# One step of a hybrid decoder layer on one core: x turned once and kept turned in DRAM, banded scores as stacked float32r products

## The chip, the cores and the metric

The kernel runs on one core of a Trainium2 chip. Its metric is the device time of one execution in microseconds (us); 0.2% of it, 3.9 us, is about what a measurement of this kernel can tell from no change. Engines: TensorE (PE) multiplies, and its weight loads are shown as PEld; VectorE (DVE) and ScalarE (ACT) do the elementwise work; GpSimd (POOL) and SyncE (SP) mostly issue DMAs. A Tile scheduler fixes the order of the instructions on each engine before the run, so each engine works strictly through its own list.

## The reference, cut to what matters

A prompt of 256 tokens and a sample group of 8 tokens go through one layer with the same weights (width 2048):

```python
def _rmsnorm(x, g):
    y = x * lax.rsqrt(jnp.mean(jnp.square(x), axis=-1, keepdims=True) + EPS)
    return y * g
# each layer
h = _rmsnorm(x, norm_mix)
q, k, v, z, xbc, dt, qm, g = jnp.split(h @ w_in, ...)
# branch A: window attention, 16 query heads of 64, 4 key/value heads, blocks of 128 positions
s = einsum('...qhgd,...khd->...hgqk', q, k) * 64 ** -0.5   # 128 queries x (previous + own block) keys
s = where(allowed, s - slopes * dist, -inf)
p = softmax with a learned sink per head
o = einsum('...hgqk,...khd->...qhgd', p, v)
# branch B: Mamba-2 SSD with a convolution; branch M: attention into 256 memory tokens
x = x + (sig(gA) * A @ w_up_swa + sig(gB) * B @ w_up_ssd + sig(gM) * M @ w_up_mem) @ w_out
x = x + (silu(h2 @ w_gate) * (h2 @ w_up)) @ w_down,   h2 = _rmsnorm(x, norm_ffn)
```

x is thus needed twice: normalized, as the input of the projections, and raw, in the residual sum after w_out.

## The kernel before

Features lie on the 128 partitions and tokens on the free axis: NT = 264 columns, 256 of the prompt (NP) and 8 of the samples (NS). The weights stream through in **units** of 512 KB, 610 of them. For each unit SP loads `raw`, ACT rounds it to float32r (`hi`, L167), DVE takes the remainder (`lo`, L168), and PE adds three float32r products for each tile of 128 features by 128 outputs, named after the PSUM bank that they fill: high by high, high by low, low by high. There are three buffers of `hi` and of `lo` and four of `raw`, so a unit is split up to three units before its products. A unit of 264 columns has 24 products.

The groups of units follow each other in the order in which they are added: memory keys and values (`pmem`, 32 units with products of 512 columns), then the input projection (`pin`): memory queries, attention queries, keys and values, gates of the memory branch, B, C, dt, then x and z of the four SSD groups between the first output projections (`pua`), then `pum`, the SSD gates, `pus`, `pout` (w_out), and the feed-forward part (`pg`, `pu`, `pdn`).

All other work is written as generators, the side tasks. After each unit the main loop lets the list `side` go on by a credit of 1.0 and the list `slow` by 0.75; each `yield` takes its number from that credit. So the numbers at the yields set at which unit a task's instructions are placed in program order; `drain` finishes a task at once where a group needs it. Program order is the scheduler's priority. Three pieces matter here:

- `prep_x` (L402 to L442) loads x, normalizes rows and turns them: for each of the 16 feature tiles k, PE turns two blocks of 128 prompt tokens and one of 8 sample tokens into PSUM (`xT`), ACT writes the high part `hh` (L439), DVE the low part `hl` (L440).
- `swa` (L785 on) computes the prompt's attention. For block 1 (256 keys) and block 0 (128 keys) and for each pair of key/value heads, PE forms scores `ps` from 64 partitions of q and of the keys kT in plain float32 (L836), DVE scales and masks them, ACT takes exponents, PE turns the probabilities (`pT`), ACT copies them to `pTa`, and PE multiplies with the values into `po` (L873): one product of 512 columns for each half a of the pair, into 64 PSUM partitions each. A plain float32 product is two PE instructions in the trace, one float32r product is one.
- `load_x` (L1447) runs ahead of each of the four `pout` groups: it loads x again, turns it again on PE (`xTr`) and copies it with ACT, for the residual sum in `after_out`.

Buffers: the pool `half` has 10 large tiles, `t1` 4 tiles of 264 columns, `ev` 4, `t4` 4; PSUM has 5 banks for the streamed groups and 3 (`sps`) for side work.

Of the kernel before, what the change touches and what calls it, by code (L numbers as in the profile page):

```python
# [8 lines left out]
F32 = mybir.dt.float32  # L9
# [9 lines left out]
P = 128  # L19
# [53 lines left out]
def tile_hybrid_decoder_step(  # L73
# [68 lines left out]
    def sps(name):  # L142
        return pq.tile([P, 512], F32, tag="s", name=nm(name))

    def mm(out, lhsT, rhs, start=True, stop=True):
        nc.tensor.matmul(out, lhsT=lhsT, rhs=rhs, start=start, stop=stop)  # L146

    def tr(out, in_):
        n = in_.shape[0]
        nc.tensor.transpose(out, in_, ident[0:n, 0:n])  # L150

    def rsqrt(v, n, parts=P, alloc=None):

# [246 lines left out]

    hh, hl = Feat("hh"), Feat("hl")

    def prep_x():
        x_t = {}
        for h in range(2):
            for t in range(2):
                m = (lm if t else ld)("x")
                nc.gpsimd.dma_start(m, x_prompt[0, t * P:(t + 1) * P, h * 1024:(h + 1) * 1024])
                x_t[t, h] = m
                yield 1.3  # L410
        xs = {h: ev("xs").rearrange("p c n -> p (c n)")[0:NS, 0:1024] for h in range(2)}
        for h in range(2):
            nc.gpsimd.dma_start(xs[h], xs_rows[:, h * 1024:(h + 1) * 1024])
            x_t[2, h] = xs[h]
        jk = t2("jkx", BF16)
        ss = tiny("ssx", 6)
        V.memset(ss, 1.0)
        for t in range(3):
            n = P if t < 2 else NS
            for h in range(2):  # L420
                act(jk[0:n], x_t[t, h], AF.Square, accum_out=ss[0:n, 2 * t + h:2 * t + h + 1])
            yield 0.5
        v = tiny("vx", 3)
        V.tensor_tensor(v, ss[:, 0:6:2], ss[:, 1:6:2], op=ALU.add)
        V.tensor_scalar(v, v, 1.0 / D, EPS, op0=ALU.mult, op1=ALU.add)
        r = rsqrt(v, 3)
        yield 1.5
        for t in range(3):
            n = P if t < 2 else NS
            for h in range(2):  # L430
                V.tensor_scalar(x_t[t, h], x_t[t, h], r[0:n, t:t + 1], None, op0=ALU.mult)
            yield 1.2
        for k in range(KT):
            ps = sps("xT")
            h, c = k // 8, (k % 8) * P
            for t in range(3):
                n = P if t < 2 else NS
# [351 lines left out]
    def swa():  # L789
# [33 lines left out]
        V.tensor_tensor(rq[:, 32:33], rq[:, 32:33], islope_c, op=ALU.mult)  # L823
        yield 3

        for blk in (1, 0):
            nk = 256 if blk else 128
            for kvp in range(2):
                halves = [slice(a * 64, a * 64 + 64) for a in range(2)]
                s = [t4("s")[:, 0:4 * nk].rearrange("p (r k) -> p r k", r=4) for _ in range(2)]  # L830
                per = 512 // nk
                for j in range(4 // per):
                    ps = [sps("ps").rearrange("p (r k) -> p r k", r=per) for _ in range(2)]
                    for i in range(per):
                        for a, rows in enumerate(halves):
                            mm(ps[a][:, i], q[rows, 4 * kvp + j * per + i, blk * P:(blk + 1) * P], kT[rows, kvp, 0:nk])  # L836
                    for a in range(2):
                        for i in range(per):
                            rr = j * per + i
                            o = blk * 16 + (2 * kvp + a) * 4 + rr  # L840
                            V.scalar_tensor_tensor(s[a][:, rr], ps[a][:, i], rq[:, o:o + 1], nd[:, 256 - nk:256],
                                                   op0=ALU.mult, op1=ALU.add)
                    yield 2.2 if blk else 2.8
                for a in range(2):
                    kv = 2 * kvp + a
                    hs = slice(kv * 4, kv * 4 + 4)
                    mx = tiny("mxa", 8)
                    V.tensor_reduce(mx[:, 0:4], s[a], axis=AX.X, op=ALU.max)
                    V.tensor_tensor(mx[:, 0:4], mx[:, 0:4], nslope[:, hs], op=ALU.mult)
                    V.tensor_tensor(mx[:, 0:4], mx[:, 0:4], nsink[:, hs], op=ALU.min)  # L850
# [12 lines left out]
                po = sps("po")  # L863
                for kb in range(nk // P):
                    pT = []
                    for a in range(2):
                        p2 = sps("pT")
                        for rr in range(4):
                            tr(p2[:, rr * P:(rr + 1) * P], s[a][:, rr, kb * P:(kb + 1) * P])
                        pT.append(t2("pTa"))  # L870
                        act(pT[a], p2, AF.Copy)
                    vb_ = blk - (nk // P - 1) + kb
                    for a, rows in enumerate(halves):  # L873
                        kv = 2 * kvp + a
                        mm(po[rows, 0:512], v_tok[:, vb_, kv * 64:(kv + 1) * 64], pT[a],
                           start=kb == 0, stop=kb == nk // P - 1)
                    yield 0.4
# [567 lines left out]
    x2 = {}  # L1445

    def load_x(i):  # L1447
        xt = t4("xg")[:, 0:1024].rearrange("p (t c) -> p t c", t=2)
        nc.gpsimd.dma_start(xt, x_prompt[0, :, 512 * i:512 * (i + 1)].rearrange("(t p) c -> p t c", p=P))
        xs = t2("xgs")[0:NS]  # L1450
        nc.gpsimd.dma_start(xs, xs_rows[:, 512 * i:512 * (i + 1)])
# [175 lines left out]
```

## Time and profile before

| what | value |
|---|---|
| median of 3 runs | 1950.66 us (1947.3 to 1951.65) |
| the profiled execution, its own time | 1951.31 us |
| its span in the trace | 1949.6 us |
| PE busy | 1927.4 us (99%), 15436 instructions |
| weight loads busy | 1863.8 us (96%) |
| DVE busy | 1160.9 us (60%) |
| ACT busy | 972.0 us (50%) |
| POOL busy | 115.2 us (6%) |
| HBM traffic | 205 GB/s over the span |

Busy times are unions over an engine's instructions. Products overlap in the pipeline, so a PE that is busy all the time may still move at different rates; the distance from start to start tells what a product takes. The span is 1.7 us shorter than the profiled execution's time.

### The profile page before, as it was taken

How to read it: one execution, taken by the hardware profiler on the slowest of the kernel's cores; microseconds unless marked ns; L12 is line 12 of the kernel's file. 1: busy time of each engine (PE TensorE's matmuls, PEld its weight loads, DVE VectorE, ACT ScalarE, POOL GpSimd, SP SyncE). 2: the span in 40 equal slices, each digit the busy share in tenths (PEclk: the TensorE clock that was granted, in tenths of full speed). 3: DMA queues.
4: the chain of work that ended last, by engine and by line, in shares of the span. 5: the costliest groups of instructions: out<-in, count | busy, mean ns of one | idle time of the engine just before them, and what ended most of it. 6: DMA issues, size and time to landing. Idle time of an engine off the chain costs nothing.

```text
span 1949.6 us, 37668 instructions
## 1 busy us (share of the span) xinstructions
PE 1927.4 (99%) x15436; PEld 1863.8 (96%) x15436; DVE 1160.9 (60%) x2217; ACT 972.0 (50%) x1420; POOL 115.2 (6%) x238
## 2 busy tenths in 40 slices
PE   8999999999999999999999999999999999999998
PEld 6799998888999999999999999999999999999998
DVE  6645577656588777677455556555445555445553
ACT  6644445655767676646444444444334444334443
POOL 3000100010001101020000000000000000000000
PEclk9999999999999999999999999999999999999999
DMA  8676676567668869788655556666566665566653
GB/s 285 195 218 207 205 221 228 184 212 244 199 201 254 285 190 320 250 294 281 180 190 188 189 163 174 183 175 185 183 182 178 182 182 180 180 183 178 181 188 128
DMA packets 191030, 400.78 MB, mean 206 GB/s; under 512 B 13443, under 2 KB 15794, under 8 KB 190720
## 3 DMA queue, kind: packets, MB, share of 16 engines
q1 hardware_dynamic: 169856, 324.13, 54.6%
q0 software_dynamic: 20848, 74.16, 11.6%
q8 instruction: 121, 1.98, 0.4%
q14 instruction: 53, 0.43, 0.1%
q10 hardware_dynamic: 152, 0.07, 0.0%
HBM read 376.53 MB, written 24.06 MB: 205 GB/s over the span
## 4 chain that ended last, share of the span: by engine, by line
PE 89%; DMA 4%; issue 3%; DVE 2%; ACT 1%; POOL 0%; SPq 0%; ACTq 0%; POOLq 0%; DVEq 0%
PE pin L146 26%; PE pu L146 13%; PE pdn L146 13%; PE pg L146 13%; PE pout L146 5%; PE pus L146 5%; PE pmem L146 5%; PE pua L146 2%; PE pum L146 1%; DMA ld<-in_state_ssm_dram 1%; PE po L146 1%; PE py L146 1%; PE ps L146 1%; DMA ld<-in_cache_mem_v_dram 1%; DMA ld<-in_cache_mem_k_dram 1%
## 5 line engine op out<-in xcount | busy, mean ns | idle before, releaser
L168 DVE TENSOR_TENSOR lo<-raw,hi 128x1024 fp32r<-128x1024 f32 (+1 forms) x626 | 747.3, 1196 | 624.5 <-ACT hi L167 623.2
L167 ACT ACTIVATE hi<-raw 128x1024 fp32r<-128x1024 f32 (+1 forms) x626 | 645.9, 1036 | 846.4 <-PE pin L146 185.5
L146 PE MATMUL pin<-hh,hi 128*128 128x264 f32 x1728 | 491.0, 287 | 2.7 <-ACT hi L167 2.7
L146 PE MATMUL pin<-hl,hi 128*128 128x264 f32 x1728 | 489.9, 286 | 0.0
L146 PE MATMUL pin<-hh,lo 128*128 128x264 f32 x1728 | 479.2, 286 | 0.7 <-DVE lo L168 0.7
L146 PEld LDWEIGHTS pin<-hh,hi 128*128 128x128 f32 x1728 | 325.2, 189 | 9.3 <-issue 4.8
L146 PEld LDWEIGHTS pin<-hl,hi 128*128 128x128 f32 x1728 | 325.3, 188 | 2.8 <-issue 2.2
L146 PEld LDWEIGHTS pin<-hh,lo 128*128 128x128 f32 x1728 | 319.1, 188 | 3.6 <-DVE lo L168 1.9
L146 PE MATMUL pdn<-fah,hi 128*128 128x264 f32 x704 | 199.7, 285 | 0.0
L146 PE MATMUL pdn<-fal,hi 128*128 128x264 f32 x704 | 199.4, 285 | 0.0
L146 PE MATMUL pu<-h2h,hi 128*128 128x264 f32 x704 | 199.4, 284 | 0.0
L146 PE MATMUL pu<-h2l,hi 128*128 128x264 f32 x704 | 199.3, 284 | 0.0
L146 PE MATMUL pg<-h2l,hi 128*128 128x264 f32 x704 | 199.1, 285 | 0.0
L146 PE MATMUL pg<-h2h,hi 128*128 128x264 f32 x704 | 198.4, 284 | 0.0
L146 PE MATMUL pdn<-fah,lo 128*128 128x264 f32 x704 | 197.0, 284 | 0.0
L146 PE MATMUL pu<-h2h,lo 128*128 128x264 f32 x704 | 196.6, 284 | 0.0
L146 PE MATMUL pg<-h2h,lo 128*128 128x264 f32 x704 | 196.1, 284 | 0.0
L146 PEld LDWEIGHTS pdn<-fah,hi 128*128 128x128 f32 x704 | 132.7, 189 | 0.1
L146 PEld LDWEIGHTS pu<-h2h,hi 128*128 128x128 f32 x704 | 132.8, 189 | 0.0
L146 PEld LDWEIGHTS pdn<-fal,hi 128*128 128x128 f32 x704 | 132.6, 188 | 0.1
L146 PEld LDWEIGHTS pu<-h2l,hi 128*128 128x128 f32 x704 | 132.7, 188 | 0.0
L146 PEld LDWEIGHTS pg<-h2h,hi 128*128 128x128 f32 x704 | 132.6, 188 | 0.0
(509 smaller groups left out, 2957.5 us busy)
## 6 DMA issues: line engine op xcount, KB each, us to landing
raw<-in_w_in_dram SPq DMA_DIRECT2D x218, 512.0 KB, 4.6
raw<-in_w_gate_dram SPq DMA_DIRECT2D x88, 512.0 KB, 3.8
raw<-in_w_up_dram SPq DMA_DIRECT2D x88, 512.0 KB, 4.4
raw<-in_w_down_dram SPq DMA_DIRECT2D x88, 512.0 KB, 4.1
raw<-in_w_mem_kv_dram SPq DMA_DIRECT2D x32, 512.0 KB, 4.9
raw<-in_w_up_ssd_dram SPq DMA_DIRECT2D x32, 512.0 KB, 3.8
raw<-in_w_out_dram SPq DMA_DIRECT2D x32, 512.0 KB, 3.6
ld<-in_cache_mem_k_dram POOLq DMA_DIRECT2D x16, 512.0 KB, 5.6
```

Source lines behind the costliest of these rows:

```text
L146: nc.tensor.matmul(out, lhsT=lhsT, rhs=rhs, start=start, stop=stop)
L167: act(hi, src, AF.Copy)
L168: V.tensor_tensor(lo, src, hi.bitcast(F32), op=ALU.subtract)
```

## The change

**x.** `prep_x` loads the 8 sample rows as one tile of 128 partitions (16 feature tiles by 8 rows) and turns that once (`xn`). Their sums of squares come from a product with a small selection matrix in the same PSUM bank. The raw prompt blocks are turned as before, two for each feature tile, and ACT copies them into `xr`, which holds raw turned x. The norm is now applied along the columns: `rb`, the reciprocal norms spread over all partitions by a product of ones with a diagonal (`rbx`), enters a DVE operation that makes `xn`; ACT then takes `hh` and DVE `hl` from it. Each `xr` (4 feature tiles) is stored to DRAM (`xT_d`), and `load_x` reads it back with one DMA, without PE and ACT.

**Attention of the prompt.** Before the scores, the keys are split in high and low parts, and each part is copied onto both halves of the partitions (`kst`). The queries of each half are split too: the high part stays on its own 64 partitions, the low part goes to the other 64 (`qst`, one tile for each half). A score tile is then two float32r products over 128 partitions, one with the high and one with the low keys, in place of one float32 product over 64 partitions. The turned probabilities of both halves now share a PSUM bank and one copy, and each value product covers 256 columns.

```diff
-        for h in range(2):
-            nc.gpsimd.dma_start(xs[h], xs_rows[:, h * 1024:(h + 1) * 1024])
+        xs = t1("xs")[:, 0:P]
+        nc.gpsimd.dma_start(xs, xs_rows.rearrange("b (k n) -> k b n", n=P))
...
+        ps = sps("xn")
+        tr(ps[:, 0:P], xs)
+        mm(ps[:, P:P + NS], ones, sel)
...
+        mm(ps[:, 0:NP], ones, dg)
+        rb = t1("rb")
...
-            for t in range(3):
-                n = P if t < 2 else NS
-                tr(ps[:, t * P:t * P + n], x_t[t, h][:, c:c + P])
-            act(hh(k), ps[:, 0:NT], AF.Copy, scale=g_mix[:, k:k + 1])
-            V.scalar_tensor_tensor(hl(k), ps[:, 0:NT], g_mix[:, k:k + 1], hh(k).bitcast(F32),
-                                   op0=ALU.mult, op1=ALU.subtract)
-            yield 0.4
+                for t in range(2):
+                    tr(ps[:, t * P:(t + 1) * P], x_t[t, h][:, o:o + P])
+                act(raw[:, c, 0:NP], ps[:, 0:NP], AF.Copy)
+                tm = t1("xn")
+                V.scalar_tensor_tensor(tm, raw[:, c], g_mix[:, k:k + 1], rb, op0=ALU.mult, op1=ALU.mult)
+                split(hh(k), hl(k), tm)
+                yield 0.6
+            nc.gpsimd.dma_start(xT_d[:, 4 * q:4 * q + 4], raw)
...
+        kst = half("kst", F32R)
+        for a in range(2):
...
+            split(kh[own], kl[own], src)
+            V.tensor_copy(kh[other], kh[own])
+            V.tensor_copy(kl[other], kl[own])
+            yield 1.0
+        qst = [half("qst", F32R) for _ in range(2)]
+        for kvp in range(2):
+            for a in range(2):
...
+                act(d[own], src, AF.Copy)
+                V.tensor_tensor(d[other], src, d[own].bitcast(F32), op=ALU.subtract)
+                yield 0.8
...
-                            mm(ps[a][:, i], q[rows, 4 * kvp + j * per + i, blk * P:(blk + 1) * P], kT[rows, kvp, 0:nk])
+                            for m in range(2):
+                                mm(ps[a][:, i], qst[a][:, 4 * kvp + j * per + i, blk * P:(blk + 1) * P],
+                                   kst[:, 4 * m + 2 * kvp + a, 0:nk], start=m == 0, stop=m == 1)
...
+                for rp in range(2):
+                    for kb in range(nk // P):
                         p2 = sps("pT")
+                        for a in range(2):
+                            for r2 in range(2):
+                                o = (2 * a + r2) * P
+                                tr(p2[:, o:o + P], s[a][:, 2 * rp + r2, kb * P:(kb + 1) * P])
+                        pT = t2("pTa")
+                        act(pT, p2, AF.Copy)
...
+                            mm(po[rows, 256 * rp:256 * rp + 256], v_tok[:, vb_, kv * 64:(kv + 1) * 64],
+                               pT[:, 256 * a:256 * a + 256], start=kb == 0, stop=kb == nk // P - 1)
+                        yield 0.4
...
-        for c in range(4):
-            ps = sps("xTr")
-            for t in range(2):
-                tr(ps[:, t * P:(t + 1) * P], xt[:, t, c * P:(c + 1) * P])
-            tr(ps[:, NP:NT], xs[:, c * P:(c + 1) * P])
-            act(o[:, c], ps[:, 0:NT], AF.Copy)
+        nc.gpsimd.dma_start(o, xT_d[:, 4 * i:4 * i + 4])
```

How the order of the instructions changes at three places. First PE, where the first `pout` group follows the last `pus` group; before:

```order
L146 MATMUL pus_12332<-sT_9950,lo_12450 128x264
L150 MATMUL xTr_12599<-ident,xg_12594 128x128 x2
L150 MATMUL xTr_12599<-ident,xgs_12596 128x8
L150 MATMUL xTr_12604<-ident,xg_12594 128x128 x2
L150 MATMUL xTr_12604<-ident,xgs_12596 128x8
L150 MATMUL xTr_12609<-ident,xg_12594 128x128 x2
L150 MATMUL xTr_12609<-ident,xgs_12596 128x8
L146 MATMUL pout_12619<-mg_11766,hi_12479 128x264 x2
```

and now, at the same place:

```order
L146 MATMUL pus_12447<-sT_10065,hi_12564 128x264 x2
L146 MATMUL pus_12447<-sT_10065,lo_12565 128x264
L146 MATMUL pout_12711<-mg_11881,hi_12594 128x264 x2
L146 MATMUL pout_12711<-mg_11881,lo_12595 128x264
L146 MATMUL pout_12712<-mg_11881,hi_12594 128x264 x2
```

The transposes are gone, here and in the other three groups. Second PE, where value products and scores of block 1 stand between `pin` products; before:

```order
L146 MATMUL pin_3503<-hh_112,lo_3410 128x264
L146 MATMUL po_3374<-pTa_3387,v_tok_2746 64x512
L150 MATMUL pT_3398<-ident,s_3071 128x128 x4
L146 MATMUL po_3374<-pTa_3396,v_tok_2746 64x512
L146 MATMUL ps_3485<-kT,qT_1739 128x256 x2
L146 MATMUL pin_3502<-hh_112,hi_3409 128x264
```

and now:

```order
L146 MATMUL pin_3497<-hl_115,hi_3706 128x264
L146 MATMUL po_3630<-pTa_3675,v_tok_2798 64x256 x2
L150 MATMUL pT_3688<-ident,s_3318 128x128
L146 MATMUL po_3630<-pTa_3684,v_tok_2798 64x256 x2
L150 MATMUL pT_3688<-ident,s_3318 128x128
L150 MATMUL pT_3688<-ident,s_3319 128x128 x2
L146 MATMUL ps_3768<-kst_3122,qst_3211 128x256 x4
L146 MATMUL pin_3497<-hh_113,lo_3707 128x264
```

A value product of 512 columns stood alone; two of 256 columns, one for each half of the partitions, now stand side by side, all twelve times. Third DVE, just before the first scores; lo_3043 and lo_3095 are the remainder of the same unit, the 82nd. Before:

```order
L168 TENSOR_TENSOR lo_3013<-raw_2980,hi_3012 128x1024
L803 COPY ssq_2941<-psq_2927 128x256
L807 MEMSET qmask_2945 128x128
L811 COPY qmask_2945<-qT_1739 64x4x8 x4
L673 ISA jks_2975,scs<-ld_2848,qb_2846 128x256
```

(three more of the last form, then lo_3043); and now, from the first of the four operations on `qst` to that unit's remainder:

```order
L860 TENSOR_TENSOR qst_3211<-qT_1791,qst_3211 64x4x256
L691 ISA jks_3027,scs<-ld_2900,qb_2898 128x256
L691 ISA scs 128x1
L851 COPY kst_3122<-kst_3122 64x2x256
L860 TENSOR_TENSOR qst_3212<-qT_1791,qst_3212 64x4x256
L691 ISA jks_3131,scs<-ld_3025,qb_3127 128x256
L691 ISA scs 128x1
L860 TENSOR_TENSOR qst_3211<-qT_1791,qst_3211 64x4x256
L691 ISA jks_3027,scs<-ld_2900,qb_2898 128x256
L691 ISA scs 128x1
L860 TENSOR_TENSOR qst_3212<-qT_1791,qst_3212 64x4x256
L168 TENSOR_TENSOR lo_3095<-raw_3062,hi_3094 128x1024
```

All ten DVE operations on `kst` and `qst` stand between the remainders of two neighbouring units; ACT's six stand likewise between the high parts of the same two units.

## Rows read from the trace of the kernel before

**Rows 1.** The page: span, busy times, granted clock by slice

```profile
span 1949.6 us, 37668 instructions
PE 1927.4 (99%) x15436; PEld 1863.8 (96%) x15436; DVE 1160.9 (60%) x2217; ACT 972.0 (50%) x1420; POOL 115.2 (6%) x238
PEclk9999999999999999999999999999999999999999
```

**Rows 2.** Waits of PE: who, for whom, us in total, times, longest

```profile
PE pv L150 <- DMA vg<-in_norm_mix_dram: 7.5, 1, 7.5
PE pin L146 <- ACT hi L167: 2.7, 3, 1.6
PE xtok L150 <- ACT xs L983: 2.0, 1, 2.0
```

**Rows 3.** Windows of pus, then pout: us, busy times, clock, DMA share, GB/s

```profile
970.45:1064.55 94.10, 94.10 (x771) 94.08 (x769) 52.23 (x72) 39.11 (x47) 1.43 (x2) 1.00 0.59 191
1064.55:1167.45 102.90, 102.90 (x819) 99.91 (x817) 55.89 (x80) 49.61 (x79) 1.42 (x2) 1.00 0.55 175
```

**Rows 4.** Timeline of PE at prep_x: start, us, instruction, count

```profile
87.15 0.38 PE L150 MATMUL xT<-ident,x 128*128 128x128 f32 x2
87.46 0.22 PE L150 MATMUL xT<-ident,xs 8*128 8x8 f32 x1
87.61 0.50 PE L146 MATMUL pmem<-lo,memh 128*128 128x512 f32 x1
```

**Rows 5.** Groups of PE by form: busy us, mean ns

```profile
L146 PE MATMUL rby<-rd,ones 128*128 128x256 f32 x8 | 2.4, 378 | 0.0
L146 PE MATMUL ps<-kT,qT 64*128 64x256 f32 x32 | 7.9, 402 | 0.0
L146 PE MATMUL ps<-kT,qT 64*128 64x128 f32 x32 | 4.0, 288 | 0.0
L146 PE MATMUL po<-pTa,v_tok 128*64 128x512 f32 x24 | 12.9, 618 | 0.0
```

**Rows 6.** Timeline of PE: scores and value products of the prompt

```profile
279.43 1.13 PE L146 MATMUL ps<-kT,qT 64*128 64x256 f32 x8
280.49 0.38 PE L146 MATMUL psT<-ones,qmask 128*128 128x1 f32 x2
...
316.81 1.07 PE L146 MATMUL po<-pTa,v_tok 128*64 128x512 f32 x2
317.82 1.13 PE L146 MATMUL ps<-kT,qT 64*128 64x256 f32 x4
318.88 0.39 PE L146 MATMUL pin<-hh,hi 128*128 128x264 f32 x1
```

**Rows 7.** Timeline of PE: value products of the samples, narrow products

```profile
395.22 0.62 PE L146 MATMUL oms<-ld,pb 128*32 128x256 f32 x2
395.77 1.07 PE L146 MATMUL po<-pTa,v_tok 128*64 128x512 f32 x2
396.78 0.62 PE L146 MATMUL oms<-ld,pb 128*32 128x256 f32 x4
397.33 1.07 PE L146 MATMUL po<-pTa,v_tok 128*64 128x512 f32 x2
...
402.74 0.95 PE L146 MATMUL sTs<-qmask,kcT 128*128 128x8 f32 x8
403.55 0.31 PE L150 MATMUL kcT<-ident,ld 128*128 128x128 f32 x1
```

**Rows 8.** Timeline before the first scores: DVE, ACT, then PE

```profile
270.41 0.67 DVE L774 TENSOR_TENSOR k_tok<-k_tok,kn_bc 128x512 f32<-128x512 f32 x1
276.24 0.42 DVE L803 COPY ssq<-psq 128x256 f32<-128x256 f32 x1 [0.34 <-PE psq L146]
279.72 1.23 DVE L168 TENSOR_TENSOR lo<-raw,hi 128x1024 fp32r<-128x1024 f32 x1 [0.44 <-ACT hi L167]
278.63 1.06 ACT L167 ACTIVATE hi<-raw 128x1024 fp32r<-128x1024 f32 x1 [0.87 <-PE pin L146]
287.20 0.39 PE L146 MATMUL pin<-hh,hi 128*128 128x264 f32 x1
```

**Rows 9.** Stretch of prep_x's transposes: window (columns as in rows 3), ACT, DVE

```profile
82.00:117.00 35.00, 35.00 (x167) 26.94 (x166) 18.45 (x25) 19.68 (x32) 3.47 (x6) 1.00 0.64 204
97.18 0.47 ACT L439 ACTIVATE hh<-xT,vgc 128x264 fp32r<-128x264 f32 x1
98.45 0.49 DVE L440 SCALAR_TENSOR_TENSOR hl<-xT,vgc,hh 128x264 fp32r<-128x264 f32 x1
```

**Rows 10.** Window from 450 to 700 us, columns as in rows 3

```profile
450.00:700.00 250.00, 245.14 (x2104) 237.21 (x2104) 182.60 (x462) 170.97 (x287) 26.46 (x37) 1.00 0.76 233
```

More of the change, by code (lines that the diff above doesn't have):

```diff
@@ L401, in tile_hybrid_decoder_step @@
     hh, hl = Feat("hh"), Feat("hl")
+    xT_d = dr.tile([P, KT, NT], F32, name="xT_d")
     def prep_x():
         x_t = {}
+        xs = t1("xs")[:, 0:P]
+        nc.gpsimd.dma_start(xs, xs_rows.rearrange("b (k n) -> k b n", n=P))
         for h in range(2):
@@ L410, in prep_x @@
                 yield 1.3
-        xs = {h: ev("xs").rearrange("p c n -> p (c n)")[0:NS, 0:1024] for h in range(2)}
-        for h in range(2):
-            nc.gpsimd.dma_start(xs[h], xs_rows[:, h * 1024:(h + 1) * 1024])
-            x_t[2, h] = xs[h]
         jk = t2("jkx", BF16)
         ss = tiny("ssx", 6)
-        V.memset(ss, 1.0)
-        for t in range(3):
-            n = P if t < 2 else NS
+        act(jk[:, 0:P], xs, AF.Square, accum_out=ss[:, 4:5])
+        for t in range(2):
             for h in range(2):
-                act(jk[0:n], x_t[t, h], AF.Square, accum_out=ss[0:n, 2 * t + h:2 * t + h + 1])
+                act(jk, x_t[t, h], AF.Square, accum_out=ss[:, 2 * t + h:2 * t + h + 1])
@@ L422, in prep_x @@
             yield 0.5
-        v = tiny("vx", 3)
-        V.tensor_tensor(v, ss[:, 0:6:2], ss[:, 1:6:2], op=ALU.add)
+        sel = tiny("sel", NS)
+        V.tensor_reduce(sel, ident.rearrange("p (k b) -> p b k", b=NS), axis=AX.X, op=ALU.add)
+        V.tensor_scalar(sel, sel, ss[:, 4:5], None, op0=ALU.mult)
+        ps = sps("xn")
+        tr(ps[:, 0:P], xs)
+        mm(ps[:, P:P + NS], ones, sel)
+        v = tiny("vx", 10)
+        V.tensor_tensor(v[:, 0:2], ss[:, 0:4:2], ss[:, 1:4:2], op=ALU.add)
@@ L425, in prep_x @@
+        V.tensor_copy(v[:, 2:10], ps[:, P:P + NS])
+        xsT = t1("xsT")[:, 0:P]
+        act(xsT, ps[:, 0:P], AF.Copy)
         V.tensor_scalar(v, v, 1.0 / D, EPS, op0=ALU.mult, op1=ALU.add)
-        r = rsqrt(v, 3)
+        r = rsqrt(v, 10)
         yield 1.5
[L428 to L437, printed above, removed]
-                tr(ps[:, t * P:t * P + n], x_t[t, h][:, c:c + P])
-            act(hh(k), ps[:, 0:NT], AF.Copy, scale=g_mix[:, k:k + 1])
-            V.scalar_tensor_tensor(hl(k), ps[:, 0:NT], g_mix[:, k:k + 1], hh(k).bitcast(F32),
-                                   op0=ALU.mult, op1=ALU.subtract)
-            yield 0.4
+        dg = t1("dgx")[:, 0:256]
@@ new lines, in prep_x @@
+        for t in range(2):
+            V.tensor_scalar(dg[:, t * P:(t + 1) * P], ident, r[:, t:t + 1], None, op0=ALU.mult)
+        ps = sps("rbx")
+        mm(ps[:, 0:NP], ones, dg)
+        rb = t1("rb")
+        act(rb[:, 0:NP], ps[:, 0:NP], AF.Copy)
+        V.tensor_copy(rb[:, NP:NT], r[:, 2:10])
+        yield 0.5
+        for q in range(4):
+            raw = ev("xr")
+            V.tensor_copy(raw[:, :, NP:NT], xsT[:, 32 * q:32 * q + 32].rearrange("p (c b) -> p c b", b=NS))
+            for c in range(4):
+                k = 4 * q + c
+                h, o = k // 8, (k % 8) * P
+                ps = sps("xT")
+                for t in range(2):
+                    tr(ps[:, t * P:(t + 1) * P], x_t[t, h][:, o:o + P])
[5 more added lines that the diff above has]
+            nc.gpsimd.dma_start(xT_d[:, 4 * q:4 * q + 4], raw)
@@ L824, in swa @@
         yield 3
+        kst = half("kst", F32R)
+        for a in range(2):
+            own, other = slice(a * 64, a * 64 + 64), slice(64 - a * 64, 128 - a * 64)
+            src = kT[own, :, 0:NP]
+            kh, kl = (kst[:, 4 * i + a:4 * i + 4:2, 0:NP] for i in range(2))
+            split(kh[own], kl[own], src)
[5 more added lines that the diff above has]
+            for a in range(2):
+                own, other = slice(a * 64, a * 64 + 64), slice(64 - a * 64, 128 - a * 64)
+                src = q[own, 4 * kvp:4 * kvp + 4, 0:NP]
+                d = qst[a][:, 4 * kvp:4 * kvp + 4, 0:NP]
+                act(d[own], src, AF.Copy)
+                V.tensor_tensor(d[other], src, d[own].bitcast(F32), op=ALU.subtract)
+                yield 0.8
         for blk in (1, 0):
@@ L863, in swa @@
                 po = sps("po")
-                for kb in range(nk // P):
-                    pT = []
-                    for a in range(2):
+                for rp in range(2):
+                    for kb in range(nk // P):
                         p2 = sps("pT")
[L868 to L877, printed above, removed]
+                        for a in range(2):
[4 more added lines that the diff above has]
+                        act(pT, p2, AF.Copy)
+                        vb_ = blk - (nk // P - 1) + kb
+                        for a, rows in enumerate(halves):
+                            kv = 2 * kvp + a
+                            mm(po[rows, 256 * rp:256 * rp + 256], v_tok[:, vb_, kv * 64:(kv + 1) * 64],
+                               pT[:, 256 * a:256 * a + 256], start=kb == 0, stop=kb == nk // P - 1)
+                        yield 0.4
                 dst = [t[:, 4 * kvp:4 * kvp + 4, blk * P:(blk + 1) * P] for t in (ah, al)]
@@ L1447, in load_x @@
     def load_x(i):
[L1448 to L1451, printed above, removed]
         o = t4("xT").rearrange("p (c n) -> p c n", c=4)
-        for c in range(4):
-            ps = sps("xTr")
-            for t in range(2):
-                tr(ps[:, t * P:(t + 1) * P], xt[:, t, c * P:(c + 1) * P])
-            tr(ps[:, NP:NT], xs[:, c * P:(c + 1) * P])
-            act(o[:, c], ps[:, 0:NT], AF.Copy)
+        nc.gpsimd.dma_start(o, xT_d[:, 4 * i:4 * i + 4])
         x2[f"r{i}"] = o
```

## Prediction

> **What bounds the kernel now.** I read the page first: PE is busy for 1927.4 of 1949.6 us, DVE for 60% and ACT for 50%, and the granted clock is full in every slice [rows 1]. Full means the upper of TensorE's two levels, 2.4 GHz. The list of PE's waits came second: the longest is 7.5 us, once, for the first vector load at the start; the next are 2.7 and 2.0 us [rows 2]. So there is hardly a wait to win, and hardly one to hide behind: what is taken from PE's list shortens the run by what it took from start to start, as long as DVE, ACT and the DMAs keep pace. Third came windows and timelines at each place that the change touches. In the window of `pus`, where nothing but weight products runs, 771 products take 94.10 us, 0.122 us each [rows 3]; that is the rate of an undisturbed stream of 264 columns.
>
> **The change part by part.**
>
> *load_x.* `pus` and `pout` each have 32 units, so 768 products of the same size. The window of `pout` takes 102.90 us, that of `pus` 94.10 [rows 3]; the 48 transposes and what they disturb are the only other PE work in it. They go: −8.8 us. What replaces them, four DMAs of 528 KB on POOL's queue, is needed only when a `pout` group ends, some 24 us after its start; ACT loses 16 copies and DVE nothing. Cover gone, a late load would delay `after_out` and, through five PSUM banks, the next group; I cost it at nothing, since the loads it replaces were as large and had to come earlier.
>
> *prep_x on PE.* The sample transposes take 0.15 us each (87.46 to 87.61), 16 of them: −2.4 us. Added are one transpose (half of 87.15 to 87.46, 0.16 us), a product with 8 columns (at most the 0.38 us of the one-column `psT`, [rows 6]) and one of 128 by 256 in float32 (2.4 us for four `rby`, 0.6 us each) [rows 4 to 6]: +1.1 us. Net −1.3 us.
>
> *Scores.* Before, the 32 instructions of 256 columns come as one batch of eight and six of four. A batch of four takes 1.06 us from its start to the next product (317.82 to 318.88), that of eight also 1.06 (279.43 to 280.49) [rows 6]: 7.4 us against 7.9 us busy in the group's row. The 128-column group has 4.0 us busy [rows 5]; in the same proportion 3.7 us. After, block 1 has 32 float32r products of 256 columns, the kind that `pin` is made of: 0.122 x 256/264 = 0.118 us each, 3.8 us. Block 0 has 32 of 128 columns, which no row shows in float32r. From below: half of 0.118, 1.9 us in all. From above: what plain float32 takes, two passes of half of 0.265 us, 8.5 us in all. The nearest row is `sTs`, 128 weights columns with only 8 columns to move, 0.101 us each (402.74 to 403.55, eight) [rows 7]: weights alone take that long, so I take 3.2 us. Scores: 11.1 − 3.8 − 3.2, −4.1 us, with ends at −5.4 and +1.2.
>
> A rule that speaks against this term: the Trainium skill, "TensorE: Matmul & The Clock Gate", section on packing small matmuls, says that products on different row groups run at the same time, so that 64-row halves cost little more than one. By it the old scores would take four batches of eight, 4.2 us, and the term would be −0.9 us. The trace agrees in the one batch of eight and disagrees in the six of four, which take as long for half the work; the rows decide.
>
> *Value products.* Before, 12 of 512 columns stand alone, two passes each, 1.01 us (395.77 to 396.78) [rows 7]: 12.1 us. After, 24 of 256 columns stand in pairs whose outputs lie on different halves of the partitions. The samples' `oms` shows this: one product of 256 columns (x2) takes 0.55 us (395.22 to 395.77), and two side by side on different output partitions (x4) take 0.55 us too (396.78 to 397.33) [rows 7]. Twelve pairs: 6.6 us, −5.5 us. If pairs don't overlap, 24 x 0.55 = 13.2, +1.1 us; I take the pair's row, since it is the same form with narrower outputs. The 48 transposes `pT` and their 12 copies stay.
>
> *Sum on PE:* −8.8 − 1.3 − 4.1 − 5.5 = −19.7 us.
>
> *What it costs DVE and ACT before the first scores.* DVE gets two operations of 512 elements (0.67 us as `k_tok`), four copies of 512 (between 0.42 and 0.84, from the copy of 256; 0.6 taken) and four of 1024 (1.2 us as `lo`): 1.3 + 2.4 + 4.8 = 8.5 us, all between two remainders. Behind them in DVE's list waits `lo` of the 82nd unit. Before, it was done at 280.95 and its unit's products began at 287.20, 6.25 us spare [rows 8]; 0.8 us of idle DVE time stands in front of it (0.34 and 0.44). PE now comes sooner, since 2.1 us of score batches ahead of that unit become 0.5. Late by 8.5 − 6.25 − 0.8 + 1.6 = 3 us: a new PE wait, +3 us. Ends: 0 (copies at the short end, ACT and DVE fully overlapped) and 6 (ACT's burst, two of 0.6 and four of 1.06 us ahead of the same unit's `hi`, adds to it).
>
> *What it costs further on.* The yields of `swa` grow by 2 x 1.0 + 4 x 0.8 for the splits and 2.4 in the value loop, 7.6 credits, so all that follows in `side` is placed about 8 units later, up to the third SSD group, where the list has caught up because it has to wait for `x` anyway. No drain is forced by that. The 8.5 us of DVE work and the displaced tasks land where DVE is busy for 182.6 of 250 us and PE already idles for 4.9 [rows 10]. I add 1.5 us, with ends 0 and 5.
>
> *prep_x on ACT and DVE.* From 82 to 117 us ACT is busy for 19.68 us and DVE for 18.45 of 35. ACT gets 16 copies of 0.47 us, DVE 16 operations of 0.49 [rows 9]: 27.2 and 26.3 of 35. PE's stream hides both; 0 taken, with an end at +3 if the chain through both engines frays.
>
> *Sum:* −19.7 + 3 + 1.5 = −15.2 us. The profiled execution took 1951.31 us, 1.7 above its span and 0.65 above the median; 1936.1 by it, 1935.5 against the median.
>
> **The rivals.**
>
> *Pairs don't overlap.* The value products keep their price: 1935.5 + 6.6 = 1942. For: their outputs share one PSUM bank, and the old scores on two row groups overlapped only in a larger batch. Against: `oms` writes one bank as well and overlaps in twos.
>
> *Narrow float32r products are dear.* Block 0 at plain float32's price: +5.3, 1941. For: no row shows them. Against: nothing but the weights row.
>
> *DVE and ACT give back what the attention saves.* Only `load_x` and `prep_x` count, −10.1, with 3 us of wait: 1943.5. For: PE idles most from 450 to 700, where DVE and ACT are busiest [rows 10]. Against: a task that comes later also meets a PE with less to do.
>
> *Slower: the chain of prep_x decides when `pin` can start.* Each feature tile now goes PE, ACT (`xr`), DVE (`xn`), ACT (`hh`), DVE (`hl`), each step at about 0.48 us in a strict list between the weight splits, with at most three `xn` tiles in flight. Before, a tile needed ACT and DVE once each. The window has 35 us for 16 tiles, 2.2 us each; every 0.1 us beyond costs PE 1.6 us. It eats the 15 us from 3.1 us a tile on; at 3.5 it costs 21 and gives 1956. For: 27 of 35 us of ACT are taken, in order, by work that waits for DVE in between. Against: the steps of one tile sum to 2.2 us, and neighbours overlap.
>
> **How the numbers follow.** Forecast 1935.5: 0.60. Narrow products dear 0.12, attention given back 0.12, pairs apart 0.08, the slower chain 0.04, and 0.04 for better than the range (no new wait, cheap narrow products: −21, 1929.5, and something unseen). The range 1927 to 1945 holds the forecast with its ends and each single rival but the chain. Below 0.2% (1946.8) lie nearly all of these: faster 0.92; two rivals together would leave no measurable change, 0.04; slower 0.04.
>
> **What would show it.** Right: no `xTr` in the trace and a window of `pout` of 94 us; pairs of `po` at 0.55 us; `ps` of 256 columns at 0.118 and of 128 at 0.10 us from start to start; one PE wait of about 3 us for `lo` or `qst` near 280 us; the start of `pin` moved by under 2 us. Wrong: `po` pairs at 1.1 us, `ps` of 128 columns at 0.2 or more, waits of PE on `hh` or `hl`, or more than 10 us of PE idle from 450 to 700.

## The result and the profile after

The changed kernel takes 1935.05 us (median of 4 runs, 1934.66 to 1942.13), the kernel before 1951.04 in the same runs: ratio 0.9926 [0.9911, 0.9942]. Five runs in a later set gave 1935.09 us and 0.9916 [0.9903, 0.9929]. The forecast was 1935.5. The number is right, in part by luck: two of its parts are wrong in opposite directions and cancel.

The profiled execution is the longest of the four, 1942.13 us. The page of the kernel after, span and busy times, against [rows 1]:

```profile
span 1940.4 us, 37644 instructions
...
PE 1908.7 (98%) x15401; PEld 1859.4 (96%) x15401; DVE 1169.8 (60%) x2246; ACT 969.6 (50%) x1423; POOL 114.1 (6%) x237
```

PE is busy 18.7 us less (1908.7 against 1927.4), but the span is only 9.2 us shorter. The waits of PE (who, for whom, us in total, times, longest) show some of the rest, against [rows 2]:

```profile
PE pmT L150 <- DVE pm L660: 3.3, 2, 3.0
PE pin L146 <- ACT hi L167: 3.0, 3, 2.4
PE pua L146 <- ACT hi L167: 2.8, 1, 2.8
PE pin L146 <- DVE lo L168: 2.6, 4, 1.0
PE ssy L146 <- ACT sqy L1239: 2.2, 2, 1.2
```

Before, no line after the start was above 2.7 us in total. Windows of the kernel after: `pus`, then `pout`, then the stretch of prep_x, then 450 to 700 us (columns as in [rows 3]):

```profile
969.92:1064.02 94.10, 94.10 (x770) 94.10 (x769) 52.06 (x71) 39.10 (x46) 1.64 (x3) 1.00 0.62 197
1064.02:1158.07 94.05, 94.05 (x771) 94.05 (x770) 56.05 (x80) 45.01 (x62) 1.61 (x3) 1.00 0.63 207
82.00:117.00 35.00, 35.00 (x205) 29.59 (x204) 26.62 (x50) 25.06 (x51) 8.07 (x15) 1.00 0.83 270
450.00:700.00 250.00, 242.53 (x2099) 233.01 (x2098) 182.65 (x476) 165.88 (x283) 27.99 (x39) 1.00 0.75 229
```

`pout` now runs at the rate of `pus`. Timeline of PE in the kernel after (start, us, instruction, count): prep_x, scores of block 1, value products with scores, scores of block 0:

```profile
88.42 0.60 PE L150 MATMUL xT<-ident,x 128*128 128x128 f32 x4
88.78 0.48 PE L146 MATMUL pmem<-hi,memh 128*128 128x512 f32 x1
...
285.41 0.64 PE L146 MATMUL ps<-kst,qst 128*128 128x256 f32 x4
285.88 0.29 PE L146 MATMUL pin<-hh,hi 128*128 128x264 f32 x1
...
333.46 0.65 PE L146 MATMUL po<-pTa,v_tok 128*64 128x256 f32 x4
334.04 0.55 PE L150 MATMUL pT<-ident,s 128*128 128x128 f32 x3
...
408.01 1.00 PE L146 MATMUL ps<-kst,qst 128*128 128x128 f32 x8
408.85 0.34 PE L146 MATMUL pin<-hl,hi 128*128 128x264 f32 x1
```

Four score products of 256 columns take 0.47 us from start to next start, 0.118 each as forecast; eight of 128 columns take 0.84, 0.105 each. A pair of value products (x4, since each is two instructions) takes 0.58, so pairs do overlap. Summed from start to next start over the whole trace, block 1's scores go from 7.4 to 4.0 us, block 0's stay at 3.7, value products go from 12.0 to 7.0: 8.4 us of PE saved in the attention.

In two places time is lost. Windows of 4 us, kernel after; the third last column is the granted clock:

```profile
208.00:212.00 4.00, 2.13 (x7) 1.82 (x8) 2.80 (x7) 3.21 (x8) 0.54 (x1) 0.64 0.47 136
212.00:216.00 4.00, 4.00 (x15) 3.52 (x14) 1.93 (x6) 0.53 (x2) 0.00 (x0) 0.51 0.80 244
216.00:220.00 4.00, 4.00 (x35) 4.00 (x35) 2.08 (x5) 1.90 (x7) 0.00 (x0) 1.00 0.05 19
...
758.00:762.00 4.00, 1.50 (x7) 1.50 (x8) 3.95 (x17) 4.00 (x11) 1.45 (x2) 0.58 0.81 280
762.00:766.00 4.00, 4.00 (x22) 4.00 (x22) 2.29 (x11) 1.76 (x4) 0.90 (x1) 0.57 0.92 210
766.00:770.00 4.00, 4.00 (x36) 4.00 (x34) 2.94 (x8) 1.94 (x2) 0.69 (x2) 1.00 1.04 355
```

At a wait of 3.0 us (over at 209.9) and one of 2.8 (over at 760.5) the granted clock falls to TensorE's lower level, 1.2 GHz: PE is busy all through 762 to 766 but starts 22 weight products there, and 36 in the 4 us behind. By the shares it stood there for 2 x 4 x (0.36 + 0.49) = 6.8 us and 2 x 4 x (0.42 + 0.43) = 6.8 us, of which some 6 and 5 lie behind the end of the wait. A weight product takes 0.22 us there from start to start in place of 0.12, so by estimate 2.2 to 2.7 us are lost on top of each wait. The first wait comes from DVE (start, us, instruction, idle before):

```profile
205.45 0.42 DVE L691 CUSTOM_DVE_ANT_0 jks<-ld,qb 128x256 f32<-128x256 f32 x1 [4.62 <-DMA ld<-in_cache_mem_k_dram]
...
206.74 0.69 DVE L650 TENSOR_REDUCE mx<-scm 128x2 f32<-128x512 f32 x1
```

A load for the samples lands late, and DVE holds the softmax of the memory attention (`mx`, then `pm`) behind it in its list.

### The profile page after: what moved, and what is told of

It reads as the page before. It is cut to its first block, busy times and chain, and to the rows that moved or that the text cites. A ratio compares the mean times of both kernels' runs of the same rounds, so it can differ in the third digit from the quotient of the medians.

```text
span 1940.4 us, 37644 instructions
## 1 busy us (share of the span) xinstructions
PE 1908.7 (98%) x15401; PEld 1859.4 (96%) x15401; DVE 1169.8 (60%) x2246; ACT 969.6 (50%) x1423; POOL 114.1 (6%) x237
## 4 chain that ended last, share of the span: by engine, by line
PE 85%; DMA 5%; issue 4%; DVE 3%; ACT 2%; POOL 0%; SPq 0%; ACTq 0%; POOLq 0%; DVEq 0%
PE pin L146 24%; PE pu L146 13%; PE pdn L146 13%; PE pg L146 13%; PE pus L146 5%; PE pout L146 5%; PE pmem L146 5%; DMA ld<-in_state_ssm_dram 2%; DVE lo L168 1%; PE pua L146 1%; ACT ld L1275 1%; DMA ld<-in_cache_mem_k_dram 1%; DVE ld L1276 1%; PE pum L146 1%; DMA raw<-in_w_in_dram 1%
```

## The experiments

All were timed in five rounds beside the kernel before; ratios are against it, with a 95% interval. "Unit" counts from 0. The change's *credits* are the yields it adds to `swa` (1.0 and 0.8 for the splits, 0.4 twice as often in the value loop); 7.6 credits in all, so the program order places the side work behind them up to 8 units later.

**e1: the change again.**

> The changed kernel once more, unaltered. In its first profile PE waited 3.0 us for the softmax of the memory attention (near 209 us) and 2.8 us for `hi` (near 758 us), and behind each wait the granted clock stood at the lower level for some 6.5 us. Theory (accident of the execution): those two waits depend on when transfers land; most executions take 1935 us, and a profile of one of those has neither wait and the clock full near 212 and 764 us. Rival (built in by the change): the waits are there in every execution of the change, a profile of a 1935 us execution shows them too, and the 7 us between executions come from somewhere else.

1935.09 us (1933.32 to 1939.93), 0.9916 [0.9903, 0.9929]; its profile is of the 1933.32 us execution. Each theory is half right. The wait near 207 us is 1.4 us there and the clock full: its length is an accident of when a load lands. The wait near 750 is there again, 2.8 us, with 6.8 us of low clock. ACT, then PE:

```profile
743.53 2.45 ACT L1275 ACTIVATE ld<-ld,dsc 128x128 f32<-128x128 f32 x8 [3.87 <-DMA ld<-in_state_ssm_dram]
745.89 1.04 ACT L167 ACTIVATE hi<-raw 128x1024 fp32r<-128x1024 f32 x1
748.36 2.45 ACT L1275 ACTIVATE ld<-ld,dsc 128x128 f32<-128x128 f32 x8 [1.42 <-DMA ld<-in_state_ssm_dram]
750.71 1.04 ACT L167 ACTIVATE hi<-raw 128x1024 fp32r<-128x1024 f32 x1
```

```profile
748.73 0.28 PE L146 MATMUL pua<-aTh,lo 128*128 128x264 f32 x1
751.80 0.59 PE L146 MATMUL pua<-aTh,hi 128*128 128x264 f32 x1 [2.80 <-ACT hi L167]
```

ACT twice waits for a state to land (3.87 and 1.42 us), scales it (2.45 us each), and only then makes the `hi` that PE needs.

**e2 and e3: one part each.** e2 is the kernel before with the hunks in `swa`, e3 with those in `prep_x` and `load_x`:

```diff
+        kst = half("kst", F32R)
...
+        qst = [half("qst", F32R) for _ in range(2)]
...
+                for rp in range(2):
+                    for kb in range(nk // P):
```

```diff
+    xT_d = dr.tile([P, KT, NT], F32, name="xT_d")
...
+            nc.gpsimd.dma_start(xT_d[:, 4 * q:4 * q + 4], raw)
...
+        nc.gpsimd.dma_start(o, xT_d[:, 4 * i:4 * i + 4])
```

> The kernel before with the attention part of the change alone (old prep_x and load_x). Theory (PE's savings add up): from the starts in the trace after, scores save 3.4 us and value products 5.0 us, at most 3 us come back as a wait near 280 us: -8.4 to -5.4, 1942.6 to 1945.6 us. Rival (given back before the SSD groups end): what is saved there is eaten by waits for DVE and ACT between 450 and 775 us, as the first profile of the change shows: 1949 to 1952 us.

> The kernel before with the x part of the change alone (prep_x and load_x new, attention old). Theory (savings add up): load_x -8.8 us by the windows, prep_x -2.6 us for the sample transposes and -2.6 us for cheaper prompt transposes (81 ns from start to start in place of 162), about +1 us for what is added: -13 us, 1938 us. As forecast (-8.8 and -1.3): 1941 us. Rival (only what is saved after 775 us counts): -8.8, 1942 us; 1942 and 1941 can't be told apart, 1938 can.

e3: 1938.18 us, 0.9928 [0.9915, 0.9940], as the theory of summed savings says. e2: 1951.85 us, 0.9995 [0.9985, 1.0004]: the attention part alone gains nothing, as its rival said. So of the change's some 17 us, x gives nearly 14.

**e4: old value products in the change.**

```diff
-                for rp in range(2):
-                    for kb in range(nk // P):
+                for kb in range(nk // P):
...
+                        mm(po[rows, 0:512], v_tok[:, vb_, kv * 64:(kv + 1) * 64], pT[a],
```

> The change with the old value products (twelve times one product of 512 columns for each half, as two copies of the turned probabilities); everything else new. Theory: 5.0 to 5.5 us more than the change, 1940 to 1940.5 us against 1935. Rival (given back anyway): no difference from the change, 1935 us; rival (the pairs were not the gain, but the smaller copies and yields were): over 6 us or under 3 us.

1947.12 us (1940.46 to 1956.38), 0.9980 [0.9965, 0.9996]: 12 us above the change, so only the last rival's "over 6 us" fits, and the runs spread widely. The profile is of the fastest run, 1940.46 us: against e1's PE is busy 4.8 us longer and idle 2.3 us longer. The other 7 us of the median stand in no profile. This kernel also has two thirds of the change's credits, so it doesn't test the value products alone; that led to the next set.

**e5 and e6: the change, and its attention part alone, with the credits out.**

```diff
-            yield 1.0
+            yield 0.0
...
-                yield 0.8
+                yield 0.0
...
-                        yield 0.4
+                        yield 0.2
```

> The whole change, but its added credits taken out: the yields of kst and qst are 0.0 in place of 1.0 and 0.8, those of the value loop 0.2 in place of 0.4, so that the sample states' work (ACT's `ld<-ld,dsc`) stands before the same units as before the change, 6 to 8 units earlier than in the change. In the change PE waits 0.75 + 2.8 us for `lo` and `hi` behind that work near 750 us, and the granted clock is low for some 6.4 us after it. Theory (the later place is what gives the attention's saving back): these waits go, -3.5 us and -3.2 us for the clock: 1928 us (1927 to 1931). Rival (the added work of DVE and ACT for kst and qst gives it back, wherever it stands): 1934 to 1936 us. Rival (DMA is full there and lets no one get ahead): the wait near 750 us goes, an equal one comes up between 700 and 800 us, 1934 to 1936 us.

> The attention part alone on the kernel before, with the added credits taken out as in the run before this one. With its credits it took 1951.85 us, no less than the kernel before. Theory (place): PE's saving of 8.6 us shows, less 1.3 us of new wait near 282 us: 1944 to 1946 us. Rivals (added work, or DMA): 1950 to 1952 us.

e5: 1939.29 us, 0.9927 [0.9914, 0.9939], no better than the change and above every range named. e6: 1949.09, 0.9981 [0.9971, 0.9991], between its ranges. The wait near 750 is gone, as theory and DMA rival said, but a longer one comes 240 us earlier (4.1 us; 3.4 in e6). e5, ACT, then PE:

```profile
497.85 0.70 ACT L1214 ACTIVATE dec<-dec,acs_tok 128x128 f32<-128x128 f32 x2 [3.87 <-DMA dec<-acs_d]
...
501.43 2.46 ACT L1275 ACTIVATE ld<-ld,dsc 128x128 f32<-128x128 f32 x8
503.90 1.28 ACT L1235 ACT_TABLE_LOAD   x1
505.20 1.09 ACT L1235 ACTIVATE z<-z 128x1056 f32<-128x1056 f32 x1
506.19 1.27 ACT L1275 ACTIVATE ld<-ld,dsc 128x128 f32<-128x128 f32 x4
507.46 1.28 ACT L1215 ACT_TABLE_LOAD   x1
508.75 1.06 ACT L1215 ACTIVATE dec<-dec 128x1024 f32<-128x1024 f32 x1
509.72 0.39 ACT L1275 ACTIVATE ld<-ld,dsc 128x128 f32<-128x128 f32 x1
510.01 1.04 ACT L167 ACTIVATE hi<-raw 128x1024 fp32r<-128x1024 f32 x1
```

```profile
506.58 0.38 PE L146 MATMUL cb<-CT,BT 128*128 128x128 f32 x2
511.10 0.59 PE L146 MATMUL pin<-hh,hi 128*128 128x264 f32 x1 [4.13 <-ACT hi L167]
```

ACT has 8.5 us of side work in one piece ahead of a `hi`, two table loads of 1.28 us among it. During that piece no DMA moves (506 to 510, windows at the end). But ahead of it ACT had stood idle 3.87 us for the load of `dec` (decays of the SSD branch, written to DRAM and read back), with all of this behind it in its list; in e9 below it waits 1.00 us for the same load. No run moves that load by itself. So the place of the side work alone isn't the cause either.

**e7 and e8: credits out, and the old scores or the old value products.**

e7's edit (kst and qst go too), then e8's:

```diff
-                            for m in range(2):
-                                mm(ps[a][:, i], qst[a][:, 4 * kvp + j * per + i, blk * P:(blk + 1) * P],
-                                   kst[:, 4 * m + 2 * kvp + a, 0:nk], start=m == 0, stop=m == 1)
+                            mm(ps[a][:, i], q[rows, 4 * kvp + j * per + i, blk * P:(blk + 1) * P], kT[rows, kvp, 0:nk])
```

```diff
-                            mm(po[rows, 256 * rp:256 * rp + 256], v_tok[:, vb_, kv * 64:(kv + 1) * 64],
-                               pT[:, 256 * a:256 * a + 256], start=kb == 0, stop=kb == nk // P - 1)
+                        mm(po[rows, 0:512], v_tok[:, vb_, kv * 64:(kv + 1) * 64], pT[a],
+                           start=kb == 0, stop=kb == nk // P - 1)
```

> As the first run of this set, but the scores in plain float32 as before (no kst and qst; value products new). Theory: 3.4 us of PE time comes back, the wait of 1.3 us near 282 us goes: 2 us above the first run of this set. As forecast: 4.1 - 3 = 1 us above. Rival (ACT's and DVE's work for kst and qst costs more further on than it saves): below the first run of this set.

> As the first run of this set, but with the old value products. Theory: 5.0 us above the first run of this set, and not the 12 us that the old value products cost against the change when their credits were left to shift. Rival (the value products are worth 12 us by themselves): 12 us above.

e7: 1934.60 us, 0.9904 [0.9891, 0.9918]. Without the new scores the kernel is 4.7 us faster than e5 (the intervals just touch), though its scores take PE 4.0 us more: the rival holds. e8: 1936.82, 0.9917 [0.9903, 0.9931], 2.5 us below e5 (0.9927) and not 5 or 12 above: theory and rival fell, and the 5 us of PE time saved by the new value products don't show in e5. Against e3, e7 is 3.7 us faster in span, though its `pin` starts 1.1 us later (unit 32): PE's saving on the value products shows there.

**e9: the query split earlier.** It becomes a side task of its own ahead of the keys' work; `kst` goes to the start of `swa`; credits out. In the traces the four splits stand 45 to 79 us earlier than in e5, more than the 30 expected.

```diff
+    def q_split():
+        q = qt["q"]
+        qst = [half("qst", F32R) for _ in range(2)]
...
+    side.add("Q", q_split(), ["q8"])
     side.add("W1", swa_keys(), ["kv"])
```

> As the change with the added credits taken out (1939.3 us), but the four splits of the queries (qst) are done some 30 us earlier, as soon as the queries are there (DVE and ACT are half idle at 230 to 260 us), and the keys' part (kst) at the start of the attention. So only 3.7 us of DVE work and 1.2 us of ACT work are left in the burst before the first scores, in place of 8.5 and 5.4. Theory (the burst pushes the chain of the attention, of the samples behind it and of dt back by several units, and PE then waits some 4 us for `hi` near 510 us with a low clock after it): that wait goes, PE's 3.4 us on the scores show: 1931 us (1930 to 1934). Rival (new scores cost by themselves, through the order of PE's list or the buffers that kst and qst hold): 1937 to 1940 us.

1929.05 us (1925.33 to 1929.95), 0.9873 [0.9858, 0.9888]: the fastest of all, clear of the change, and a little better than the theory's range. Its rival (the order of PE's list, or the buffers that kst and qst hold) is out, since the new scores are still there and qst is held for longer. No wait near 510, none near 750. e9, ACT, the work that blocked PE in e5:

```profile
481.30 2.45 ACT L1226 ACTIVATE dec<-dec,acs_tok 128x128 f32<-128x128 f32 x8 [1.00 <-DMA dec<-acs_d]
483.65 1.04 ACT L167 ACTIVATE hi<-raw 128x1024 fp32r<-128x1024 f32 x1
484.60 0.97 ACT L1287 ACTIVATE ld<-ld,dsc 128x128 f32<-128x128 f32 x3
485.47 1.04 ACT L1227 ACTIVATE dec<-dec 128x1024 f32<-128x1024 f32 x1
486.42 3.90 ACT L1287 ACTIVATE ld<-ld,dsc 128x128 f32<-128x128 f32 x13
490.23 2.94 ACT L167 ACTIVATE hi<-raw 128x1024 fp32r<-128x1024 f32 x3
```

The same work, some 20 us earlier, with the `hi` between made in time.

**e10: old scores, but kst and qst still built and used by nothing.**

Against e7:

```diff
+        kst = half("kst", F32R)
...
+        qst = [half("qst", F32R) for _ in range(2)]
...
+                act(d[own], src, AF.Copy)
+                V.tensor_tensor(d[other], src, d[own].bitcast(F32), op=ALU.subtract)
```

> As the kernel with new value products and old float32 scores (1934.6 us), but with kst and qst still computed, in the same place, and used by nothing. Theory (burst): no gain of PE, all of the burst's cost: 3.4 + 4.7 = 8 us above that kernel, 1942 us (1939 to 1944). Rival (the new scores themselves): 1934 to 1936 us.

1934.45 us, 0.9913 [0.9899, 0.9926], against e7's 0.9904: the theory (8 us) fell. The burst's work on DVE and ACT costs at most a few us by itself; it costs more only where the scores wait for it, and not always there (e8, below).

**e11: the new value products alone, on the kernel before.**

```diff
-                        mm(po[rows, 0:512], v_tok[:, vb_, kv * 64:(kv + 1) * 64], pT[a],
-                           start=kb == 0, stop=kb == nk // P - 1)
-                    yield 0.4
...
+                            mm(po[rows, 256 * rp:256 * rp + 256], v_tok[:, vb_, kv * 64:(kv + 1) * 64],
+                               pT[:, 256 * a:256 * a + 256], start=kb == 0, stop=kb == nk // P - 1)
+                        yield 0.2
```

> The kernel before with the new value products alone (yields of 0.2, so that the later work stands before the same units; prep_x, load_x and scores old). Theory (PE's savings add up where no DVE or ACT work comes with them): 5.0 us less than before, ratio 0.9974. Rival (the value products' saving needs the x part to show, as the whole attention part did): ratio 0.999 to 1.001.

1946.39 us, 0.9966 [0.9954, 0.9979]: the theory's 0.9974 lies inside, the rival is out.

**e12: e9 with credits.**

```diff
-            yield 0.0
+            yield 1.0
...
-                        yield 0.2
+                        yield 0.4
```

> The early split of the queries (1929.05 us with the added credits taken out), with the change's credits back where they can be: 1.0 after each half of kst, 0.4 in the value loop, so that the work behind the attention stands 3 to 4 units later. It tells whether a later place costs by itself once the scores no longer wait for the split. Theory (it was the late chain, not the place): 1927 to 1931 us, no waits of 2 us or more between 280 and 775 us. Rival (place): a wait of 2 to 3 us for `hi` or `lo` behind the sample states' work near 745 us, with a low clock behind it, comes back: 1933 to 1936 us.

1938.05 us, 0.9920 [0.9907, 0.9934]: the theory fell; a later place costs by itself, 9 us, more than the rival's 1933 to 1936 us. And the rival's wait near 745 isn't what came: the longest, 2.8 us, is over at 507.8, two for `lo` come near 635. The waits of PE in e12:

```profile
PE pin L146 <- DVE lo L168: 4.3, 3, 1.9
PE pin L146 <- ACT hi L167: 3.5, 2, 2.8
```

Together, with the unit that PE was in when the last value product started and when ACT's `dec` came up (from the traces), and with PE's idle time (span less busy time, from the pages):

```
kernel                      last po   dec    PE idle   us        ratio to before
    the kernel before       u107      u134   22.2
e3  x only, old attention   u107      u134   21.7      1938.18   0.9928 [0.9915, 0.9940]
e11 values only, old x      u110      u134   22.6      1946.39   0.9966 [0.9954, 0.9979]
e7  old scores, no credits  u110      u134   22.4      1934.60   0.9904 [0.9891, 0.9918]
e8  as e5, old values       u111      u134   24.1      1936.82   0.9917 [0.9903, 0.9931]
e10 burst, old scores       u113      u134   22.6      1934.45   0.9913 [0.9899, 0.9926]
e9  early, no credits       u113      u134   22.9      1929.05   0.9873 [0.9858, 0.9888]
e12 early, credits          u115      u137   30.6      1938.05   0.9920 [0.9907, 0.9934]
e4  as e1, old values       u114      u137   29.3      1947.12   0.9980 [0.9965, 0.9996]
e5  late, no credits        u119      u138   30.3      1939.29   0.9927 [0.9914, 0.9939]
e6  as e5, old x            u119      u138   27.2      1949.09   0.9981 [0.9971, 0.9991]
e1  the change              u121      u139   27.0      1935.09   0.9916 [0.9903, 0.9929]
e2  as e1, old x            u121      u139   28.2      1951.85   0.9995 [0.9985, 1.0004]
```

Where `dec` stays at unit 134, PE is idle for 22 to 24 us, and the attention's saving on PE shows (e7, e10 and e11 have only the value products' share, e8 only the scores'). Where it comes 3 to 5 units later, by a late chain or by credits, PE is idle for 27 to 31 us: it waits for `hi` or `lo` behind side work, in each kernel at another place. e9, e5 and e12 show the price most plainly: PE is busy for 1904.0, 1904.9 and 1905.1 us in them, so nearly all of the 8 to 9 us between their spans is idle time of PE.

Split and credits make a square: late with credits 0.9916, late without 0.9927, early with 0.9920, early without 0.9873. Either one alone gives the saving back; only the early split with the later work held in place keeps it. The lateness stands in ACT's list, fixed before the run: ahead of the first `dec` the list has the `hi` of 136 or 137 units where `dec` comes up in unit 134, and of 139 to 141 in the others.

What isn't settled: why the late split puts `dec` late with the new value loop (e5) and not with the old one (e8), whose scores wait for it just the same; why the change, late on both counts, does a little better than e5 (their intervals overlap); and what makes e4 spread.

## Why the prediction was right, point by point

The total came out because two errors cancel. Against the kernel before, the start of a unit's first product moved by (us, from the traces):

```
unit               40      80      122     142     210     218     282     346     end
x only (e3)       -4.0    -4.2    -5.3    -5.3    -2.6    -2.6    -4.6   -13.5   -13.4
change (e1)       -4.7    -6.2   -23.5   -15.9   -13.2    -6.6    -9.2   -18.0   -18.0
early split (e9)  -2.9    -2.6   -18.0   -12.9   -11.6   -11.6   -13.9   -22.8   -22.8
```

- *load_x, -8.8 us: right.* From the start of `pus` (unit 282) to the end of `pout` (346) every kernel with it gains 8.8 to 8.9 us.
- *prep_x, -1.3 us: right in kind, too small.* It gave about 4 us, more than half of it where I had counted nothing: the prompt's transposes went from 5.2 to 2.6 us (32 of them, 162 ns to 81 from start to start). The forecast took their price as unchanged, though [rows 4] has two in 0.31 us with a small one behind; four in a row now take 0.36. x as a whole: 13.8 us against 10.1 forecast.
- *Scores, -4.1 on PE: nearly right (-3.4).* 256 columns as forecast. The 128 columns cost 0.115 us each over all 32, nearer to the weights' row than to any other, 3.7 us against 3.2. The Trainium skill, "TensorE: Matmul & The Clock Gate", section on packing small matmuls, says that products on different row groups run at the same time; by that the term would have been an estimated -0.9. The trace agrees: in the old batch of eight, with both halves, the instructions start in pairs 0.01 us apart. The prediction read the six batches of four as disagreeing. They don't bear on it: such a batch fills one `ps` tile (the order before shows `ps_3485` alone), so it has one half and one row group, and its instructions start 0.22 us apart. The term by the rows was right because the scheduler had kept the halves apart, not because they can't overlap.
- *Value products, -5.5: right.* 5.0 us by starts; e11 measures 6.6 us for them alone (0.34% [0.21, 0.46]).
- *Costs of the attention, +4.5 us: size nearly right, place wrong.* These are the steps that failed. "Late by 8.5 − 6.25 − 0.8 + 1.6 = 3 us: a new PE wait, +3 us": the wait came, but at 1.3 us (unit 81; start to next start, both profiles of the change). "I add 1.5 us, with ends 0 and 5": of 8.4 us saved 3.1 were left, so some 4 us went further on, and between units 210 and 218 alone the change gives 6.6 us back. The sum also took a wait at its length; behind the one of 2.8 us near 750 the lower clock took an estimated 2.2 us more. What I missed is the chain behind the attention (samples, dt, the states): with split and credits as they are it stands later in the lists, and each list that mixes it with weight splits hands the lateness to PE. I did say that later work "also meets a PE with less to do"; it met a PE that had come earlier, which is the opposite of cover.
- *The rival "DVE and ACT give back what the attention saves"* (0.12) is thus the better half of the truth on the attention: attention gives 3.1 us in the medians (e1 against e3, intervals overlapping) of 8.4 saved, and none alone. The time was right because x gave 3.7 us more than forecast and the attention some 2 less.
- *Pairs apart, narrow products dear, prep_x's chain:* excluded by the rows above. From 82 to 117 us ACT is busy 25.1 and DVE 26.6 us, near the 27.2 and 26.3 forecast, and `pin` starts (unit 32) 2.9 us earlier, not later; the sign "moved by under 2 us" missed.
- *"More than 10 us of PE idle from 450 to 700"* didn't come: 7.5 us [rows 10: 4.9].

## What to carry to other kernels

When an engine that bounds the kernel is relieved, look at what the relief asks of the others *and who waits for it*: 8.4 us saved on PE, part of it by preparing operands on DVE and ACT, were worth about 3 us as the change stood, and all of it (9.3 us of span, e9 against e3) once the preparation was moved 45 to 79 us ahead into half idle engines and the later work was kept in its place. Time taken from a stream that nobody waits on (`load_x`, the transposes) came through whole. In a kernel with fixed lists, test an edit with the places of the later work held still, and then move them: three units cost 9 us here (e12 against e9).

## What the runs showed of the hardware

- A wait of PE can cost more than its length, but its length alone doesn't tell. At those of 2.8 (twice), 3.0 and 4.1 us shown above the granted clock was at 1.2 GHz for 6.8 us each time, 5 to 6 us of them behind the wait, an estimated 2.2 to 2.7 us of PE's work lost besides. At one of 2.8 us in e12 (over at 507.8) it was there for 3.4 us, and at one of 1.6 us in e9 (over at 593.8) for 3.4 us too; behind the 2.4 us in the first profile of the change (over at 612.6) and the 1.4 us in e1 it stayed full. The windows of e5 around the wait that ends at 511.1, then one each of e12, e9 and the first profile of the change:

```profile
506.00:510.00 4.00, 0.97 (x9) 0.77 (x7) 0.18 (x1) 3.98 (x8) 0.00 (x0) 0.95 0.00 0
510.00:514.00 4.00, 2.90 (x13) 2.90 (x14) 2.88 (x4) 3.83 (x7) 0.00 (x0) 0.50 0.16 31
514.00:518.00 4.00, 4.00 (x29) 3.86 (x30) 2.38 (x3) 1.06 (x1) 0.00 (x0) 0.70 0.78 247
...
507.00:511.00 4.00, 3.23 (x16) 3.24 (x17) 4.00 (x6) 2.61 (x3) 0.00 (x0) 0.65 0.08 14
...
594.00:598.00 4.00, 4.00 (x21) 4.00 (x22) 3.72 (x7) 1.19 (x2) 0.86 (x2) 0.57 0.99 332
...
612.00:616.00 4.00, 3.45 (x34) 3.14 (x35) 4.00 (x14) 3.97 (x5) 1.44 (x2) 1.00 0.31 102
```

- The mean granted clock of an execution goes with it: 0.996 in the one of 1942.13 us, 0.998 and 0.999 in the three others of the change.
- Plain float32 products on 64 partitions overlap in pairs when the two halves alternate in PE's list (starts 0.01 us apart), and take 0.22 us an instruction from start to start when one half stands alone (256 columns, two instructions a product, kernel before).
- A float32r product of 128 columns takes 0.105 to 0.115 us, hardly less than one of 256 (0.118 to 0.124): halving the columns saves next to nothing here.
